# Moving two of three modulation sums from TensorE to VectorE in a hybrid decoder layer

## The chip, the cores and the metric

The kernel runs on one core of a Trainium2 chip. The core has five engines with queues of their own, each worked through in order: TensorE (PE, matrix products; its weight loads are shown as PEld), VectorE (DVE), ScalarE (ACT), GpSimd (POOL) and SyncE (SP), which here issues all transfers from the chip's memory. The metric is the device time of one execution in microseconds; lower is better.

## The reference, cut to what matters

One layer of a decoder: 256 tokens of width 2048. A conditioning vector c gives six modulations of 2048 numbers each, by one product of silu(c) with a matrix of 2048 x 12288:

```python
mod = (silu(c) @ w_mod + b_mod).reshape(B, 6, D)
sh1, sc1, g1, sh2, sc2, g2 = [mod[:, i, None, :] for i in range(6)]

h = rmsnorm(x, norm_mix) * (1.0 + sc1) + sh1
proj = h @ w_in                       # inputs of four mixers
y = concat([gla, gated_deltanet, pooling, forgetting_attention]) @ w_out
x = x + g1 * y

h = rmsnorm(x, norm_ffn) * (1.0 + sc2) + sh2
x = x + g2 * conv_ffn(h)              # gate, up: 2048 x 5632; down: 5632 x 2048
out = rmsnorm(x, norm_final)
```

Everything is float32. The first two modulations are needed at once. g1 is needed when the output projection is done, sc2 and sh2 at the second norm, g2 at the very end. This case is about when, and on which engine, the middle ones (g1, sc2, sh2) are summed.

## The kernel before, in words

Large products are made from split operands: each block of weights (128 x 1024 numbers, tile wr) is cut by ScalarE into a high part (wh) and by VectorE into the rest (wl), and three products of the parts stand for one product in float32. `load_split` (line 158) does one load and its split. The buffers allow five wr, three wh and three wl at a time.

The layer goes through these stages. First, the modulations sh1 and sc1 are summed in four groups while the input projection for DeltaNet follows group by group (tile acc). The projections for the other mixers, called `extras`, go by pairs of column blocks (tile ext); the last group of them, 25 steps, runs beside the mixers. The function `gated_deltanet` is traced first and so comes first where engines are contended; then, in the order "gpfd", the extra projections that a mixer needs and the mixer itself: GLA, pooling, attention (`fox`), and the finish of DeltaNet. Their products are in the tiles gdt (DeltaNet) and oxt (the others). Then comes the output projection, in five column chunks (`project`, three of 512 and two of 256 wide; 32 loads in all; sums in ext, oxt, wot, ext and oxt), then the second norm and the feed-forward part (tile fpt), which takes the second half of the time.

One half modulation is 1024 columns and is called by a letter and a number: s is sc2, h is sh2, g is g1; s0 is the first half of sc2. `gemv` (line 178) sums one, in eight steps of two loads of 512 KB each (tile wm, four buffers, shared by both ways). There are two ways:

- On TensorE: four matmuls per step with the conditioning number as weights of 32 columns, into the PSUM tile bgt, of which there is one. ScalarE copies the sums to a wr buffer and eight short products with `sel` finish them.
- On VectorE: two instructions `ga = wm * cond + ga` over 128 x 1024 per step (line 103, from line 174), into the SBUF tile ga, of which there is one. Then products with `ones` sum over the partitions: eight short ones for s and h, or four of 512 columns for g, which make a row.

Lists say which half goes which way, and rates how many steps of each are traced per step of the extra projections:

```python
ON_PE, PE_RATE = "s0 s1 h0", 0.38
ON_DVE, DVE_RATE = "h1 g0 g1", 0.69
```

`paced` gives out these steps. What is left of both lists is traced after the mixers, the TensorE list first (the flush). A g half has a condition before its row is formed: its mixer (GLA for g0, attention for g1, whose value tiles gv and fv the rows take over) must have been traced, and the TensorE list must be finished ("s" in `emitted`). Until then a step of it does nothing.

The order on every engine is fixed when the program is built. A planner goes through the instructions by priority, which is the order of tracing except where `high_priority` lifts the end of a modulation, and starts each on a simulated clock when its inputs and a buffer are there. So a step traced at one place fills gaps that lie near it. The transfers of the modulations are held behind an earlier one on SyncE's queue (`issue_after`), and are otherwise put into that queue in the planned order.

Of the kernel before, what the change touches and what calls it, by code (L numbers as in the profile page):

```python
# [49 lines left out]

ORDER = "gpfd"

ON_PE, PE_RATE = "s0 s1 h0", 0.38
ON_DVE, DVE_RATE = "h1 g0 g1", 0.69


def _consts():
# [16 lines left out]
def trunk_kernel(ctx: ExitStack, tc: tile.TileContext, x, c, w_mod, b_mod, norm_mix, norm_ffn, w_in,  # L74
# [36 lines left out]
    def act(o, a, f, **kw):  # L111
        S_.activation(o, a, f, **kw)
# [115 lines left out]
    with ExitStack() as ph:  # L228
# [59 lines left out]
        with ExitStack() as st:  # L288
# [184 lines left out]
                    yield from pair(p, done[p], g + 1)  # L473
                    done[p] = g + 1

            def jobs(seq, pst):
                col = pst or (ext)
                for job in seq.split():
                    kind, n = job[0], int(job[1])
                    k0, col0 = 8 * n, dict(s=4, h=3, g=2)[kind] * D + n * 1024  # L480
                    if kind == "s":
                        yield from gemv(col0, to_col(s2, 4, k0, nffn, col), pst)
                    elif kind == "h":
                        yield from gemv(col0, to_col(sh2, 3, k0, None, col), pst)
                    else:
                        yield from gemv(col0, g1_row(n, bgt), None,
                                        lambda: "gf"[n] in emitted and "s" in emitted, b_mod[:, col0:col0 + 1024])
# [3 lines left out]
            def marked(steps):  # L491
                yield from steps
                emitted.add("s")
# [10 lines left out]

            bgt = lambda: bgp.tile([P, 512], F32, name="bgt", tag="bgt")
            bg = [marked(jobs(ON_PE, bgt)), jobs(ON_DVE, None)]
            for _ in mods(0):
                pass
            hold = [last_wm[0]]
# [334 lines left out]
                finish(onl[t], t, nw_gla, 4, oxt().rearrange("p (h n) -> p h n", n=P))  # L844


        def fox(fp):
            ft_ = lambda shape, name, bufs=1: fp.tile(shape, F32, name=name, tag=name, bufs=bufs)
            fq, fk = pr[:, 16:20], pr[:, 20:24]
            for h in range(4):  # L850
                la = ft_([P, 3, P], "la", 2)
                for i, (m_, t) in enumerate(((K(K_LE), 0), (K(K_LE), 1), (ones, 0))):
                    act(la[:, i], m_, AF.Copy, scale=fl[:, t, h:h + 1])
                pT = oxt()
                ptv = pT[:, 0:3 * P].rearrange("p (a n) -> p a n", n=P)
                for t in range(NT):
                    n = (t + 1) * P
                    b = oxt()
                    mm(b[:, 0:n], fq[:, h, t * P:t * P + P], fk[:, h, 0:n], stop=False)
                    if t == 0:  # L860
                        mm(b[:, 0:n], la[:, 0], K(K_GT), start=False, stop=False)
                    else:
                        mm(b[:, 0:n], la[:, 1], K(K_ONE, 2 * P), start=False, stop=False)
                        mm(b[:, 0:P], la[:, 2], K(K_GT), start=False, stop=False)
                    mm(b[:, n - P:n], idr, ngr, start=False)
                    p = ft_([P, 2 * P], "p", 3)
                    s4 = ft_([P, 4], "s4", 3)
                    V.tensor_reduce(out=s4[:, 0:1], in_=b[:, 0:n], axis=AX.X, op=ALU.max, negate=True)
                    act(p[:, 0:n], b[:, 0:n], AF.Exp, bias=s4[:, 0:1], accum_out=s4[:, 1:2])
                    V.reciprocal(out=s4[:, 2:3], in_=s4[:, 1:2])  # L870
                    act(p[:, 0:n], p[:, 0:n], AF.Copy, scale=s4[:, 2:3])
                    for kk in range(t + 1):
                        PE.transpose(ptv[:, t + kk if kk == 0 else 2], p[:, kk * P:kk * P + P], ident)
                pt = ft_([P, 3, P], "pt", 2)
                S_.copy(pt, ptv)
                b = oxt()
                hs = slice(h * P, h * P + P)
                mm(b[:, 0:T], fv[:, 0, hs], flat(pt[:, 0:2]), stop=False)
                mm(b[:, P:T], fv[:, 1, hs], pt[:, 2], start=False)
                S_.copy(fq[:, h], b[:, 0:T])  # L880


        def pooling(pp):
            pw = pp.tile([P, 4, P], F32, name="pw")
            nc.sync.dma_start(pw, pool_w[0].rearrange("g c d -> c g d"))
            u = pr[:, 12:16]
            sa, sb = pp.tile([P, 4, T], F32, name="sa"), pp.tile([P, 4, T], F32, name="sb")
            cur, nxt = u, sa
            for li in range(4):
                sh = 1 << li  # L890
                S_.copy(nxt[:, li:, 0:sh], cur[:, li:, 0:sh])
                tt(nxt[:, li:, sh:], cur[:, li:, sh:], cur[:, li:, 0:T - sh], ALU.add)
                w = 2 * sh
                dl = pp.tile([P, T], F32, name="dl", tag="dl", bufs=2)
                hd = pp.tile([P, 16], F32, name="hd", tag="hd", bufs=2)
                stt(dl, nxt[:, li], 1.0 / w, u[:, li], ALU.mult, ALU.subtract)
                tt(hd, nxt[:, li, 0:16], K(K_INV + 16 * li, 16), ALU.mult)
                tt(dl[:, 0:16], hd, u[:, li, 0:16], ALU.subtract)
                b = oxt()
                mm(b[:, 0:T], pw[:, li], dl)  # L900
                act(u[:, li], b[:, 0:T], AF.Copy, scale=pscale[:, li:li + 1])
                cur, nxt = nxt, (sb if nxt is sa else sa)
# [44 lines left out]
        chunks = ((0, 512), (512, 512), (1024, 512), (1536, 256), (1792, 256))  # L947
        Y2 = bigA()

        def project(n, a):  # L950
            c0, w = chunks[n]
            nk = 1024 // w
            for j in range(KT // nk):
                ks = order[nk * j:nk * j + nk]
                if n == 0:
                    for k in ks:
                        split(Y2[:, k, 0:T], Y2[:, k, T:], pr[:, k + 4])
                wh, wl = load_split(wo_v, ks[0], nk, c0, w)
                steps = [(kk, k, t) for kk, k in enumerate(ks) for t in range(NT)]
                if n == len(chunks) - 1 and ks[-1] == order[-1]:  # L960

                    steps.sort(key=lambda s: s[2])
                for kk, k, t in steps:
                    st, sp_ = j + kk == 0, nk * j + kk == KT - 1
                    xh, xl = Y2[:, k, t * P:t * P + P], Y2[:, k, T + t * P:T + t * P + P]
                    mm(a[t], xh, wh[:, kk], start=st, stop=False)
                    mm(a[t], xh, wl[:, kk], start=False, stop=False)
                    mm(a[t], xl, wh[:, kk], start=False, stop=sp_)
# [12 lines left out]
        with tc.tile_pool(name="op", bufs=2, reuse_waits="tile") as op:  # L981
            for n, (c0, w) in enumerate(chunks):
# [6 lines left out]
                for t in range(NT):  # L989
                    m_ = op.tile([P, 512], F32, name="m_", tag="m_")[:, 0:w]  # L990
                    tt(m_, a[t], g1t[c0 // 1024][:, gs], ALU.mult)
                    tt(x1[:, t, ns], x1[:, t, ns], m_, ALU.add)
                    act(m_, x1[:, t, ns], AF.Square, accum_out=x1s[:, t, n:n + 1])


    with ExitStack() as ph:
# [150 lines left out]
```

## Time and profile before

| | |
|---|---|
| median of 3 runs | 1301.3 us (1297.34 to 1302.14) |
| the profiled execution | 1299.62 us |
| its span, first to last instruction | 1297.8 us |
| mean granted TensorE clock | 0.985 |
| TensorE busy | 1243.1 us (96%) |
| TensorE weight loads busy | 1075.8 us (83%) |
| VectorE busy | 889.1 us (69%) |
| ScalarE busy | 636.2 us (49%) |
| moved by DMA | 311.91 MB, mean 240 GB/s |

The profile is one execution. Busy times of an engine are sums over its instructions. A row of a group gives line, engine, operation, output tile and input tiles, shapes and count, then busy time in us and the mean of one in ns, then the idle time just before them and what ended it. "A <- B" in the view of waits means that A waited for B, with total us, times and the longest. The chain of work that ended last is followed back from the last instruction, at each step to what released it.

### The profile page before, as it was taken

Reading aid. Unit: us, or ns where it says so; the run is one execution under the profiler, and the core shown is the slowest. Engines: PE = TensorE matmul, PEld = TensorE weight load, DVE = VectorE, ACT = ScalarE, POOL = GpSimd, SP = SyncE. Lnnn points to the kernel's source line nnn. Section 1 sums busy time; section 2 is a strip of 40 time slices with the busy share of each in tenths; the row PEclk is TensorE's granted clock in tenths of the full one; section 3 lists DMA queues with packets and bytes.
Section 4 is the critical chain, followed back from the end, with each engine's and each line's share of the span. In section 5 each row is a group of like instructions: output and inputs, shape, how many; then the busy total and the mean of one; then the engine's idle time right before and its main releaser. Section 6 shows DMA issues by size and latency. Waiting matters only on the chain.

```text
span 1297.8 us, 19845 instructions
## 1 busy us (share of the span) xinstructions
PE 1243.1 (96%) x7663; PEld 1075.8 (83%) x7663; DVE 889.1 (69%) x1201; ACT 636.2 (49%) x1000; POOL 23.1 (2%) x31
## 2 busy tenths in 40 slices
PE   2799999999999999999999999999999999999995
PEld 1799999898876688888888888888888888888884
DVE  7679797989763397676657666665666587964543
ACT  3455344774354454564545545554545444443432
POOL 0200000010000100000000000000000000000000
PEclk9799999999999999999999999999999999999998
DMA  9899999796567898556576666657665699875552
GB/s 326 274 367 377 333 333 302 255 334 227 163 231 248 306 330 279 155 165 192 163 212 193 179 196 194 182 172 209 186 191 165 212 364 379 307 259 184 193 194 81
DMA packets 168597, 311.91 MB, mean 240 GB/s; under 512 B 16172, under 2 KB 54067, under 8 KB 167863
## 3 DMA queue, kind: packets, MB, share of 16 engines
q1 hardware_dynamic: 168503, 310.65, 73.0%
q8 instruction: 60, 0.98, 0.3%
q14 instruction: 34, 0.28, 0.1%
HBM read 308.51 MB, written 2.10 MB: 239 GB/s over the span
## 4 chain that ended last, share of the span: by engine, by line
PE 91%; DMA 4%; SPq 1%; DVE 1%; ACT 1%; issue 1%; POOLq 0%; ACTq 0%; DVEq 0%
PE fpt L97 57%; PE ext L97 16%; PE oxt L97 5%; PE acc L97 4%; PE gdt L97 4%; DMA wm<-in_w_mod_dram 3%; PE bgt L97 3%; PE wot L97 2%; DMA wr<-in_w_in_dram 1%; DVE ga L103 1%; ACT xT L1015 0%; SPq L155 0%; SPq L399 0%; DVE m L100 0%; DVE wl L100 0%
## 5 line engine op out<-in xcount | busy, mean ns | idle before, releaser
L100 DVE TENSOR_TENSOR wl<-wr,wh 128x1024 fp32r<-128x1024 f32 x384 | 469.4, 1223 | 293.7 <-ACT wh L115 292.9
L115 ACT CAST wh<-wr 128x1024 fp32r<-128x1024 f32 x384 | 403.6, 1051 | 489.5 <-PE fpt L97 316.5
L97 PE MATMUL fpt<-bigA,wh 128*128 128x512 f32 x1408 | 399.6, 396 | 2.1 <-DVE bigA L103 2.1
L97 PEld LDWEIGHTS fpt<-bigA,wh 128*128 128x128 f32 x1408 | 239.2, 189 | 32.9 <-issue 2.2
L97 PEld LDWEIGHTS fpt<-bigA,wl 128*128 128x128 f32 x1408 | 222.6, 188 | 34.2 <-DVE wl L100 3.7
L97 PE MATMUL fpt<-bigA,wl 128*128 128x256 f32 x1408 | 240.5, 279 | 0.0
L103 DVE SCALAR_TENSOR_TENSOR ga<-wm,cond,ga 128x1024 f32<-128x1024 f32 x139 | 178.1, 1281 | 11.5 <-DMA wm<-in_w_mod_dram 10.6
L97 PE MATMUL fpt<-wl,AH 128*128 128x512 f32 x352 | 137.5, 391 | 0.0
L97 PE MATMUL ext<-bigA,wh 128*128 128x256 f32 x768 | 137.3, 281 | 0.0
L97 PE MATMUL fpt<-wh,AL 128*128 128x512 f32 x352 | 137.0, 389 | 0.0
L97 PE MATMUL fpt<-wh,AH 128*128 128x512 f32 x352 | 123.5, 390 | 0.0
L97 PEld LDWEIGHTS ext<-bigA,wh 128*128 128x128 f32 x768 | 117.5, 189 | 3.0 <-DVE dS L100 0.8
L97 PE MATMUL ext<-bigA,wl 128*128 128x256 f32 x384 | 107.4, 280 | 1.7 <-DVE wl L100 1.7
L97 PE MATMUL ext<-wh,bigA 128*128 128x256 f32 (+1 forms) x384 | 79.3, 300 | 0.0
L97 PEld LDWEIGHTS fpt<-wh,AH 128*128 128x128 f32 x352 | 66.1, 188 | 14.1 <-ACT wh L115 0.2
L97 PEld LDWEIGHTS fpt<-wl,AH 128*128 128x128 f32 x352 | 66.1, 188 | 13.9 <-DVE m L100 0.2
L97 PEld LDWEIGHTS fpt<-wh,AL 128*128 128x128 f32 x352 | 66.1, 188 | 13.8 <-issue 0.2
L97 PE MATMUL acc<-bigA,wh 128*128 128x256 f32 x384 | 70.1, 289 | 4.6 <-ACT bigA L115 2.7
L97 PEld LDWEIGHTS ext<-bigA,wl 128*128 128x128 f32 x384 | 72.1, 188 | 2.8 <-DVE wl L100 1.9
L97 PEld LDWEIGHTS ext<-wh,bigA 128*128 128x128 f32 x384 | 61.6, 188 | 5.5 <-ACT wh L115 1.7
L97 PEld LDWEIGHTS acc<-bigA,wh 128*128 128x128 f32 x384 | 60.7, 199 | 5.0 <-ACT bigA L115 2.8
L97 PE MATMUL ext<-wl,bigA 128*128 128x256 f32 (+1 forms) x192 | 58.3, 304 | 1.6 <-DVE wl L100 1.6
(344 smaller groups left out, 1172.1 us busy)
## 6 DMA issues: line engine op xcount, KB each, us to landing
wm<-in_w_mod_dram SPq DMA_DIRECT2D x192, 512.0 KB, 5.7
wr<-in_w_in_dram SPq DMA_DIRECT2D x88, 512.0 KB, 9.1
wr<-in_ffn_w_gate_dram SPq DMA_DIRECT2D x88, 512.0 KB, 3.9
wr<-in_ffn_w_up_dram SPq DMA_DIRECT2D x88, 512.0 KB, 4.4
wr<-in_ffn_w_down_dram SPq DMA_DIRECT2D x88, 512.0 KB, 4.4
wr<-in_w_out_dram SPq DMA_DIRECT2D x32, 512.0 KB, 4.8
xt<-in_x_dram SPq DMA_DIRECT2D x2, 1024.0 KB, 7.1
bigC<-in_x_dram SPq DMA_DIRECT2D x2, 1024.0 KB, 12.2
```

Of the source, the lines that this page charges most:

```text
L97: PE.matmul(o, lhsT=l, rhs=r, start=start, stop=stop, skip_group_check=True)
L100: V.tensor_tensor(out=o, in0=a, in1=b, op=op)
L103: V.scalar_tensor_tensor(out=o, in0=a, scalar=s, in1=b, op0=op0, op1=op1)
L115: S_.copy(hi, src)
```

## The change: what it does

The list of TensorE keeps s0, at a rate of 0.25 steps per step of the extra projections in place of 0.38. The half s1 joins VectorE's list behind h1; the rate of that list stays. New places give out steps of that list: two before each of the four attention heads, one before each of the four steps of pooling. The half h0 is summed on VectorE during the output projection: from the second column chunk on, one of its eight steps is traced at every third load of output weights; its column sums go through the tile bgt. Nothing else of the computation is changed.

```diff
-ON_PE, PE_RATE = "s0 s1 h0", 0.38
-ON_DVE, DVE_RATE = "h1 g0 g1", 0.69
+ON_PE, PE_RATE = "s0", 0.25
+ON_DVE, DVE_RATE = "h1 s1 g0 g1", 0.69
+LATE, LATE_LOADS = "h0", 3
...
-            def jobs(seq, pst):
-                col = pst or (ext)
+            def jobs(seq, pst, col=None):
+                col = col or pst or ext
...
             bg = [marked(jobs(ON_PE, bgt)), jobs(ON_DVE, None)]
+            late = jobs(LATE, None, bgt)
...
+        def beside(n):
+            with tc.issue_after(hold[0].ins):
+                for _ in range(n):
+                    next(bg[1], None)
+
         def fox(fp):
...
             for h in range(4):
+                beside(2)
...
         def pooling(pp):
...
             for li in range(4):
+                beside(1)
...
+        wo_loads = [0]
+
         def project(n, a):
...
                 wh, wl = load_split(wo_v, ks[0], nk, c0, w)
+                wo_loads[0] += 1
+                if n > 0 and wo_loads[0] % LATE_LOADS == 0:
+                    next(late, None)
...
+        for _ in late:
+            pass
```

## The prediction

> **What bounds the kernel now.** I read the engine totals first, then the chain of work that ended last, then the busy time stage by stage, and last who issues and who waits in the stages that the change touches.
>
> ```profile
> span 1297.8 us, 19845 instructions
> PE 1243.1 (96%) x7663; PEld 1075.8 (83%) x7663; DVE 889.1 (69%) x1201; ACT 636.2 (49%) x1000; POOL 23.1 (2%) x31
> PE 91%; DMA 4%; SPq 1%; DVE 1%; ACT 1%; issue 1%; POOLq 0%; ACTq 0%; DVEq 0%
> PE fpt L97 57%; PE ext L97 16%; PE oxt L97 5%; PE acc L97 4%; PE gdt L97 4%; DMA wm<-in_w_mod_dram 3%; PE bgt L97 3%; PE wot L97 2%; DMA wr<-in_w_in_dram 1%; DVE ga L103 1%; ACT xT L1015 0%; SPq L155 0%; SPq L399 0%; DVE m L100 0%; DVE wl L100 0%
> ```
>
> TensorE sets the end: 91% of the chain is its work. Its modulations (tile bgt) hold 3% of that chain, about 40 us. Nothing else that the change touches has as much to give. The next question is whether TensorE is full where bgt stands. The columns are busy time and count by engine, granted clock, share of the DMA engines, rate.
>
> ```profile
> core 0: us, PE busy (x) PEld busy (x) DVE busy (x) ACT busy (x) POOL busy (x), PEclk, DMA share, GB/s
> 245.00:381.00 136.00, 135.39 (x1105) 118.75 (x1108) 112.77 (x175) 70.82 (x141) 6.74 (x4) 1.00 0.72 242
> 381.00:445.00 64.00, 63.53 (x427) 40.07 (x416) 24.15 (x70) 29.39 (x84) 1.01 (x1) 1.00 0.78 261
> 445.00:462.00 17.00, 17.00 (x84) 13.32 (x82) 10.00 (x17) 12.80 (x32) 2.75 (x2) 1.00 0.98 372
> 462.00:505.00 43.00, 43.00 (x190) 35.32 (x189) 42.43 (x42) 19.50 (x26) 0.00 (x0) 1.00 0.92 334
> 505.00:541.00 36.00, 36.00 (x249) 32.92 (x249) 19.98 (x22) 15.82 (x22) 0.96 (x1) 1.00 0.63 189
> by line: PE bgt L97 40.1%; PE gdt L97 31.7%; PE oxt L97 15.4%; DMA wm<-in_w_mod_dram 6.1%; PE oxt L873 2.8%; PE gdt L672 1.7%; PE gdt L661 1.4%; PE gdt L656 1.3%; PE gdt L735 0.4%; issue 0.1%
> ```
>
> Stage 1 (245 to 381) has the last extra input projections, GLA and the first half of DeltaNet. Stage 2 (381 to 445) has the rest of DeltaNet, pooling and most of the attention, and no projection matmuls at all. Stage 3 (445 to 541) is the output projection. TensorE is full in all three. The last line is the chain from 381 to 448: bgt is its largest single part, 40.1%. VectorE is busy for 24.15 of 64 us there, so there is room for the moved work just where TensorE has none.
>
> **The change, part by part.** *What leaves TensorE.*
>
> ```profile
> L97 PE MATMUL bgt<-wm,cond 128*32 128x512 f32 x192 | 38.0, 603 | 1.1 <-DMA wm<-in_w_mod_dram 1.1
> L97 PE MATMUL bgt<-wm,cond 128*32 128x512 f32 x120 | 24.5, 603 | 0.5 <-DMA wm<-in_w_mod_dram 0.5
> L97 PE MATMUL bgt<-sel,wr 128*128 128x1 f32 x32 | 3.9, 252 | 0.0
> ```
>
> The first row is all three jobs; the other two are of stage 2 alone. A job has 8 steps of two loads, so 192 records are 24 steps of 8. Stage 2 holds 120 of them, 15 steps at 24.5/15 = 1.63 us; stage 1 the other 9 steps at (38.0 - 24.5)/9 = 1.50 us. That agrees with the pace in the code: 25 steps of extra projections (counted from the loop) times 0.38 is 9.5, so 9 steps are paced and 15 are left for the flush. With one job at 0.25, 6 steps are paced and 2 flushed. So stage 1 loses 3 steps, 4.5 us, and stage 2 loses 13, 21.2 us: **25.7 us** of TensorE in all (two thirds of 38.0 gives 25.3). The short column sums (bgt<-sel, 3.9/2 us a job) stay: s1 and h0 need the same eight products from ga and ones. The two copies of bgt to wr vanish on ScalarE, which is not full.
>
> *What VectorE gets.* Two jobs of 16 accumulations each.
>
> ```profile
> core 0: us, PE busy (x) PEld busy (x) DVE busy (x) POOL busy (x), PEclk, DMA share, GB/s
> 245.00:381.00 136.00, 1.95 (x16) 1.86 (x16) 33.32 (x26) 0.96 (x1) 1.00 0.72 242
> 381.00:445.00 64.00, 0.00 (x0) 0.00 (x0) 0.00 (x0) 0.00 (x0) 1.00 0.78 261
> 445.00:541.00 96.00, 4.09 (x8) 1.49 (x8) 20.49 (x16) 1.90 (x2) 1.00 0.82 286
> L103 DVE SCALAR_TENSOR_TENSOR ga<-wm,cond,ga x16: 1277/1280/1285, 462.6 to 503.6; 128x1024 f32<-128x1024 f32 x16
> L97 PE MATMUL bgt<-ga,ones x8: 591/592/594, 445.7 to 515.1; 128*128 128x512 f32 x8
> POOL ga L179 <- PE bgt L97: 61.3, 1, 61.3
> ```
>
> These are the windows of the tile ga alone. One accumulation takes 1.28 us, so the two jobs add 32 x 1.28 = 41 us to VectorE. Now h1 and g0 run in stage 1 and g1 runs from 462.6 to 503.6. In between there is nothing for 61.3 us: the one ga buffer holds g0 until its row is formed, and that waits for the flush of TensorE's three jobs (the code marks "s" only then). With 2 steps to flush instead of 15, g0's row can be formed soon after 381, and g1 can move into stage 2.
>
> The order is then: 17 paced steps and 4 in pooling (h1, s1, part of g0), then the first steps before the attention heads finish g0 (of the 8 offered there, some find g0 already waiting), then g1 in the flush. In stage 1 the paced amount is the same 17 steps, and 136 - 112.77 = 23 us are free, enough for four more steps (10 us). Stage 2 gets about 8 accumulations of g0 and 16 of g1, 31 us on top of 24.15: 55 us.
>
> *The late job, h0.* Its 8 steps stand at every third of the 24 loads behind the first column chunk, so it adds 16 x 1.28 = 20.5 us to stage 3, which is what g1 (20.49 us) leaves if it moves forward.
>
> ```profile
> 472.70:494.70 22.00, 22.00 (x98) 18.07 (x97) 21.46 (x21) 9.79 (x12) 0.00 (x0) 1.00 1.01 375
> ```
>
> This window is the second chunk, 8 loads of weights. VectorE is 97.5% busy with about one accumulation per load, DMA moves 375 GB/s, and TensorE misses nothing. The late job asks for two accumulations per three loads, less than that. I cost it at 0. If g1 stayed where it is, h0 could not begin before the last row product has read ga, at 515.1; then 20.5 us come onto the 19.98 in 505 to 541, 40.5 in 36, and the second norm starts 4.5 us late. So the bounds are 0 and +4.5, and I take 0 because the row that runs denser costs nothing. The additions to the projection's SyncE queue are 16 loads of wm among 24 of wr; the row above has the same mixture.
>
> *What stage 2 really gives back.* If TensorE alone set it, 64 us would shrink by 21.2 to 42.8. Two things can hold it longer. The first is the loads.
>
> ```profile
> 381.50 56.94 SPq L185 DMA_DIRECT2D wm<-in_w_mod_dram  x30
> 438.49 5.01 SPq L155 DMA_DIRECT2D wr<-in_w_out_dram  x5
> wm<-in_w_mod_dram SPq DMA_DIRECT2D x192, 512.0 KB, 5.7
> DMA to landing us min/median/max: 3.6/4.8/8.1
> ```
>
> SyncE issues 30 wm loads there and only then the first load of the output weights. After the change: 4 loads for TensorE, about 8 for g0, 16 for g1 and 8 of output weights for the first chunk, 36 x 0.524 MB = 18.9 MB. At the 375 GB/s of the row above that is 50 us, so stage 2 can shrink by 14 at most before the loads bind, unless g1 spills into stage 3, where there is room. The second is the two chains, DeltaNet's and the attention's, each of which passes TensorE, then VectorE or ScalarE, and TensorE again; without filler TensorE waits in them. There is new filler: half of the first chunk (GLA's and pooling's heads, 4 of 8 loads, half of 22 us = 11 us) needs neither chain, and with the 26 wm loads gone from ahead of it, its weights can come early. The bounds of stage 2's gain are 0 (only chains) and 21.2 (only TensorE); I take **14**, the loads' bound, which also leaves TensorE 7 us of waits.
>
> The trace shows what empty stretches can do to the clock:
>
> ```profile
> 545.00:549.00 4.00, 1.81 (x10) 1.51 (x11) 2.70 (x7) 3.06 (x8) 0.00 (x0) 1.00 0.34 117
> 549.00:553.00 4.00, 4.00 (x17) 3.40 (x16) 2.26 (x5) 2.12 (x5) 0.00 (x0) 0.57 0.00 0
> ```
>
> After four microseconds at 1.81 busy, the granted clock was 0.57 in the next four. Stage 2 would have 7 idle us spread over some 40 hops, far from 1.81 of 4, so I add nothing; one such dip costs about 4 x 0.43 = 1.7 us. [...]
>
> *Sum.* Stage 1: -4.5, of which VectorE at 112.77 of 136 may keep 1.5, so -3. Stage 2: -14. Stage 3: 0. Together **-17 us**. The profiled execution took 1299.62 us, of which 1297.8 span; less 17 it is 1282.6. The median of the runs is 1.7 above it, so **1284 us** is the forecast.
>
> **The rivals.** *Full gain.* TensorE sets everything, as its 63.53 of 64 us suggest: the whole 25.7 comes back, 1301.3 - 25.7 = 1276. The filler of 11 us speaks for it, the loads against. Chance 0.12.
>
> *The chains set stage 2.* The bgt pieces only fill what DeltaNet and the attention leave open; taken away, TensorE idles there. For it: weight loads are busy for 40.07 of 64 us in stage 2 against 118.75 of 136 in stage 1. Against it stands the chain itself, in order of time (start, length):
>
> ```profile
> 424.67 0.99 PE bgt L97 x8
> 425.66 1.02 PE gdt L97 x8
> 426.68 0.98 PE bgt L97 x4
> ...
> 429.07 1.08 PE gdt L97 x8
> 430.16 0.99 PE bgt L97 x8
> 431.15 0.58 PE gdt L97 x4
> 431.73 0.98 PE bgt L97 x4
> ```
>
> DeltaNet's pieces (gdt) each have a bgt piece of about 1 us ahead of them or behind, so the chains may well wait for bgt. In this case only stage 1's 3 to 4.5 us are left, 1297. [...] Chance 0.17.
>
> *VectorE stands in the chains' way: slower.* VectorE's queue is in order. An accumulation whose wm is late holds DeltaNet's and the attention's operations queued behind it, and TensorE behind those.
>
> ```profile
> DVE ga L103 <- DMA wm<-in_w_mod_dram: 2.9, 4, 1.6
> ```
>
> Before, such waits are 2.9 us in stages 1 to 3. The 30 loads of stage 2 came every 56.94/30 = 1.9 us, with four buffers and 4.8 us to land; at this pace a step of two takes 3.8 us, of which VectorE works 2.56 and could wait 1.24. Over the 14 steps of wm in stage 2 that is 17 us put onto chains which, in this case, no longer gain from bgt's absence. Less stage 1's 4.5 that is +12.5: 1314. It decides once these waits pass 4.5 us, and it shows from 11. Chance 0.10.
>
> **How the numbers follow.** The forecast's own case (gain 10 to 23, 1278 to 1291) gets 0.61. What a measurement of this kernel tells from no change is about 0.5%, 6.5 us. Forecast and full gain are faster by more: 0.73; of the chains' case (gain 0 to 9) 0.05 is faster, 0.11 within, 0.01 slower; of the slower case 0.01 is within and 0.09 slower. So faster 0.78, same 0.12, slower 0.10. The range goes from 1274, just under the full gain, to 1299, which takes in the chains' case and leaves out the slower one.
>
> **What would show it.** Right: the group bgt<-wm,cond has 64 records and some 12 to 13 us; ga runs at 381 to 445 where its window was empty, and its last 16 accumulations, of h0, lie among the output projection; the first output weights are issued well before 438, and projection matmuls (ext<-wh,bigA) stand between DeltaNet's; TensorE stays at 95% or more from the end of the extra projections to the second norm. Wrong: if TensorE falls to 70% in that stretch with releasers DVE or ACT, the chains set it; if VectorE's waits for wm pass 10 us, the slower case; if g1 still ends near 500 after the shift, h0 crowds the end of stage 3 and the second norm starts late.

## The result and the profile after

| | before | after |
|---|---|---|
| median of 15 runs each | 1301.15 us (1297.34 to 1303.63) | 1313.82 us (1300.73 to 1317.44) |
| ratio, 95% interval | 1 | 1.0082 [1.0065, 1.0099] |
| TensorE busy, profiled execution | 1243.1 us | 1224.1 us |
| VectorE busy, profiled execution | 889.1 us | 923.9 us |
| span and clock of the profiled execution | 1297.8 us, 0.985 | 1299.0 us, 0.980 |

The kernel became 0.8% slower, where 1.3% faster was forecast; the time lies outside the range. One thing has to be known for reading the profile: the profiled execution of the changed kernel is the quickest of its 15, 13 us under their median. It shows what became of the work; what the other executions lost is seen only beside a second profile of the same kernel (the first experiment). Medians and intervals in this document leave out four executions whose whole program ran far slower (one of f1's ten, 2069.78 us at a clock of 0.556, one of f2's nine, 1566.75 us at 0.742, and two of the kernel before beside e1 to e4).

The totals of the changed kernel's page, and the shares of its chain of waits by engine:

```profile
span 1299.0 us, 19653 instructions
PE 1224.1 (94%) x7535; PEld 1073.5 (83%) x7535; DVE 923.9 (71%) x1233; ACT 636.2 (49%) x998; POOL 22.7 (2%) x31
PE 76%; DMA 9%; DVE 8%; ACT 3%; issue 2%; SPq 1%; POOL 0%; ACTq 0%; POOLq 0%; DVEq 0%
```

TensorE does 19 us less and the span is no shorter: its share of the chain fell from 91% to 76%, and DMA and VectorE now hold 17%. The same five stretches as in the prediction (busy time and count by engine, granted clock, DMA share, rate):

```profile
245.00:381.00 136.00, 129.51 (x1065) 118.99 (x1065) 120.65 (x185) 71.86 (x141) 6.84 (x4) 0.97 0.76 243
381.00:445.00 64.00, 56.55 (x353) 44.65 (x352) 52.89 (x93) 32.03 (x77) 0.98 (x2) 0.97 0.85 289
445.00:462.00 17.00, 11.29 (x61) 8.04 (x56) 9.94 (x23) 10.29 (x35) 2.03 (x2) 1.00 0.78 295
462.00:505.00 43.00, 41.54 (x177) 33.08 (x178) 39.81 (x39) 19.05 (x26) 0.00 (x0) 1.00 0.82 293
505.00:541.00 36.00, 36.00 (x267) 33.84 (x267) 19.91 (x25) 15.30 (x21) 0.95 (x1) 1.00 0.63 190
```

TensorE was full in all of them before. Now it stands empty for 6.5 us in stage 1, 7.5 in stage 2, 5.7 in the next 17 us and 1.5 in the 43 behind: 21 us, where 27.6 us of bgt left it. The accumulations on VectorE (tile ga alone, without ScalarE's column) moved the way that the prediction gave:

```profile
core 0: us, PE busy (x) PEld busy (x) DVE busy (x) POOL busy (x), PEclk, DMA share, GB/s
245.00:381.00 136.00, 3.69 (x32) 3.73 (x32) 44.09 (x35) 0.95 (x1) 0.97 0.76 243
381.00:445.00 64.00, 2.15 (x4) 0.60 (x4) 23.03 (x18) 0.95 (x1) 0.97 0.85 289
445.00:541.00 96.00, 4.09 (x20) 2.53 (x20) 23.78 (x19) 0.95 (x1) 1.00 0.74 255
```

Stage 2, which held none, holds 18 (about 24 were given). The group of TensorE's modulations, the output weights' issues on SyncE's queue, and the waits of VectorE's accumulations for their loads (245 to 541) follow, each from its own view:

```profile
L99 PE MATMUL bgt<-wm,cond 128*32 128x512 f32 x64 | 10.4, 603 | 3.7 <-DMA wm<-in_w_mod_dram 3.7
```

```profile
401.70 1.41 SPq L157 DMA_DIRECT2D wr<-in_w_out_dram  x3
```

```profile
DVE ga L105 <- DMA wm<-in_w_mod_dram: 6.3, 5, 2.7
```

64 records are left, the output weights start 37 us sooner (401.70 against 438.49), and VectorE waits 6.3 us for loads against 2.9. In this execution the second norm's first instruction stood at 545.3 us, against 545.8 before. Everything was moved as described, and nothing was gained.

### The profile page after: what moved, and what is told of

It reads as the page before. It is cut to its first block, busy times and chain, and to the rows that moved or that the text cites. A ratio compares the mean times of both kernels' runs of the same rounds, so it can differ in the third digit from the quotient of the medians.

```text
span 1299.0 us, 19653 instructions
## 1 busy us (share of the span) xinstructions
PE 1224.1 (94%) x7535; PEld 1073.5 (83%) x7535; DVE 923.9 (71%) x1233; ACT 636.2 (49%) x998; POOL 22.7 (2%) x31
## 4 chain that ended last, share of the span: by engine, by line
PE 76%; DMA 9%; DVE 8%; ACT 3%; issue 2%; SPq 1%; POOL 0%; ACTq 0%; POOLq 0%; DVEq 0%
PE fpt L99 57%; PE ext L99 10%; DMA wm<-in_w_mod_dram 4%; DMA wr<-in_w_in_dram 4%; PE oxt L99 3%; DVE ga L105 3%; PE acc L99 2%; DVE wl L102 2%; PE gdt L99 2%; PE wot L99 2%; DMA wr<-in_w_out_dram 1%; ACT wh L117 1%; DVE xt L105 1%; PE bgt L99 1%; DMA wsm<-in_w_in_dram 0%
## 5 line engine op out<-in xcount | busy, mean ns | idle before, releaser
L105 DVE SCALAR_TENSOR_TENSOR ga<-wm,cond,ga 128x1024 f32<-128x1024 f32 x169 | 216.1, 1279 | 15.3 <-DMA wm<-in_w_mod_dram 13.0
```

The source lines that it names most:

```text
L105: V.scalar_tensor_tensor(out=o, in0=a, scalar=s, in1=b, op0=op0, op1=op1)
```

## The experiments

Ratios are against the kernel before, on the same chip. The clock and the span are medians over the runs of each kernel; the last column is worked out (see "One kernel, twice").

| run | what differs | us | ratio [95%] | clock | span | span at 0.985 |
|---|---|---|---|---|---|---|
| before | | 1301.15 | | 0.985 | 1299.3 | 1299 |
| after | | 1313.82 | 1.0082 [1.0065, 1.0099] | 0.969 | 1312.0 | 1296 |
| e1 | the changed kernel again | 1311.79 | 1.0085 [1.0058, 1.0111] | 0.968 | 1310.0 | 1293 |
| e2 | s1's part alone | 1326.28 | 1.0188 [1.0153, 1.0223] | 0.967 | 1324.5 | 1307 |
| e3 | h0's part alone | 1300.48 | 0.9993 [0.9974, 1.0011] | 0.9815 | 1298.7 | 1295 |
| e4 | s1 and h0 left out | 1299.75 | 0.999 [0.9972, 1.0008] | 0.980 | 1297.9 | 1293 |
| e5 | after, with empty TensorE steps | 1331.53 | 1.0215 [1.0193, 1.0238] | 0.972 | 1329.8 | 1317 |
| e6 | short accumulations of s1 and h0 | 1301.05 | 0.9989 [0.9974, 1.0004] | 0.9795 | 1299.3 | 1294 |
| e7 | TensorE's rate back at 0.38 | 1301.25 | 0.999 [0.9977, 1.0003] | 0.976 | 1299.5 | 1291 |
| e8 | e4, with empty TensorE steps | 1306.88 | 1.0038 [1.0019, 1.0057] | 0.982 | 1305.1 | 1302 |
| e9 | s0 and s1 on TensorE, rate 0.64 | 1308.69 | 1.0049 [1.0026, 1.0072] | 0.981 | 1306.9 | 1303 |
| e10 | before, with 21 forced gaps | 1468.09 | 1.1288 [1.1258, 1.1318] | 0.940 | | |
| e11 | rates 0.38 and 0.48 | 1302.53 | 1.0011 [0.9998, 1.0024] | 0.977 | 1300.75 | 1293 |
| e12 | before, TensorE's rate 0.25 | 1308.37 | 1.0067 [1.0043, 1.009] | 0.984 | 1306.6 | 1306 |
| f1 | rates 0.25 and 0.48 | 1306.94 | 1.0047 [1.0028, 1.0065] | 0.974 | 1305.2 | 1294 |
| f2 | no steps between attention and pooling | 1306.78 | 1.0043 [1.0029, 1.0057] | 0.974 | 1305.0 | 1294 |
| f3 | rates 0.38 and 0.58 | 1303.57 | 1.0018 [1.0003, 1.0033] | 0.977 | 1301.8 | 1294 |
| f4 | rates 0.50 and 0.58 | 1304.24 | 1.002 [1.0006, 1.0034] | 0.9775 | 1302.4 | 1295 |

**One kernel, twice.** e1 is the changed kernel with no edit.

> The changed kernel once more, to see a profile of an ordinary execution: its own profile took 1300.7 us, while its runs had a median of 1313.8 and their granted clock fell with their time (0.980 at a span of 1299.0, 0.964 to 0.972 at 1308 to 1316). Theory A, the clock: TensorE's waits in the stages of the mixers let the granted clock dip; an execution near 1313 shows more or longer stretches below 1.00 between 245 and 560 us, the same busy times of the other engines, and a time that is longer by about its loss of mean clock times the span. Theory B, VectorE's queue alone: the time differs between executions because VectorE's waits for loads differ; an execution near 1313 shows some 13 us more of DVE waits for wm, and the clock is a by-product.

The loss repeats, and the clock goes with it. Over the 21 executions of the changed kernel in both sets of runs, spans run from 1299.0 us at a clock of 0.980 to 1315.7 at 0.966, on a straight line of -984 us per 1.0 of clock (correlation -0.94). The last column of the table is the median span moved to 0.985 with this slope; it is an extrapolation, no measurement. It is good to some 3 us at best: the same kernel comes out at 1296 in one set and at 1293 in the other, and the slopes within other kernels differ (-933 in e4, -539 in e6, -765 in e7). e1's profiled execution had a span of 1315.3 us. Around the place where it parts from the other one, first in the profile of the first run, then in e1's (same columns as above):

```profile
320.00:324.00 4.00, 3.90 (x37) 3.64 (x36) 4.00 (x8) 1.70 (x4) 0.00 (x0) 1.00 0.84 253
324.00:328.00 4.00, 1.46 (x13) 1.49 (x14) 4.00 (x7) 0.95 (x3) 0.00 (x0) 1.00 0.31 74
328.00:332.00 4.00, 3.19 (x30) 2.81 (x28) 4.00 (x7) 2.81 (x6) 0.00 (x0) 1.00 0.40 115
...
340.00:344.00 4.00, 4.00 (x28) 3.75 (x29) 2.74 (x7) 0.42 (x1) 0.95 (x1) 0.73 0.40 129
```

```profile
324.00:328.00 4.00, 1.91 (x20) 1.65 (x18) 4.00 (x6) 1.30 (x4) 0.00 (x0) 0.88 0.43 144
328.00:332.00 4.00, 3.47 (x16) 3.49 (x16) 3.94 (x7) 0.59 (x1) 0.00 (x0) 0.50 0.43 135
332.00:336.00 4.00, 4.00 (x22) 3.67 (x21) 1.78 (x3) 1.89 (x5) 0.00 (x0) 0.50 0.42 131
336.00:340.00 4.00, 4.00 (x23) 3.66 (x21) 3.22 (x8) 0.62 (x2) 0.00 (x0) 0.50 0.42 131
340.00:344.00 4.00, 4.00 (x18) 3.77 (x19) 3.43 (x5) 1.60 (x4) 0.00 (x0) 0.50 0.71 186
344.00:348.00 4.00, 4.00 (x38) 3.93 (x37) 2.99 (x6) 1.39 (x3) 0.00 (x0) 0.93 0.64 207
348.00:352.00 4.00, 4.00 (x20) 3.78 (x20) 0.85 (x4) 0.00 (x0) 0.95 (x1) 0.50 0.00 1
352.00:356.00 4.00, 4.00 (x23) 3.88 (x23) 2.90 (x3) 0.59 (x1) 0.00 (x0) 0.50 0.14 22
356.00:360.00 4.00, 4.00 (x19) 3.66 (x18) 1.73 (x2) 1.69 (x3) 0.00 (x0) 0.50 0.71 245
360.00:364.00 4.00, 4.00 (x31) 3.82 (x30) 1.99 (x3) 1.05 (x1) 0.00 (x0) 0.86 0.40 133
364.00:368.00 4.00, 4.00 (x32) 3.59 (x30) 3.87 (x7) 1.63 (x5) 0.00 (x0) 1.00 0.43 131
```

Both lose TensorE for over 2 us at 324 to 328, and VectorE is busy throughout. TensorE's longest wait on VectorE at 320 to 332 is the same, for the tile W of DeltaNet (total, times, longest; again the first run's profile, then e1's):

```profile
PE gdt L99 <- DVE W L639: 2.6, 1, 2.6
```

```profile
PE gdt L99 <- DVE W L639: 3.4, 2, 2.6
```

In the first the clock stays at 1.00 behind it and is 0.73 and 0.84 in two later windows (340 to 348). In e1 it is 0.50 in seven of the nine windows from 328 to 364, though TensorE is busy for 4.00 of 4 from 332 on: x16 to x23 instructions in such a window, against x32 at 364, at 1.00. Taking each window's length times what its clock lacks to 1.00, 324 to 364 lost 15.3 us of clock in e1 and 1.7 us in the first, and the last matmul of the extra projections starts at 399.6 against 387.0, 12.6 us later. Over 184 to 620 the lost clock is 28.9 against 8.5 us, a difference of 20.4; the spans differ by 16.3. Before, the same sum was 1.7 us. VectorE's waits for wm are 5.4 us in e1 and 6.3 in the first, so late loads are not what sets the two apart. The difference between two executions of this kernel is clock. What sets it off is not shown: the fall in e1 begins at a gap, but the quicker execution has the longer idle time at the same place (2.54 against 2.09 of 4 us) and kept 1.00, and f1 below shows a fall without any gap.

Summed over windows of 4 us, the falls lose close to whole multiples of 1.7 us of clock: 1.72, 1.72, 1.68 and, at 544 to 556, 3.40 in the first profile; 15.32 at 324 to 364 and else 1.68, 1.72, 1.68, 3.40 and 3.40 up to 548 in e1's; 5.12 at 308 to 324 in f1's and 6.84 at 324 to 344 in e7's. What sets this length is not shown.

**The two parts apart, and no work at all.** e2 leaves h0 on TensorE and sums only s1 on VectorE, with the steps between; e3 does only h0 beside the output projection.

```diff
 e2
-ON_PE, PE_RATE = "s0", 0.25
+ON_PE, PE_RATE = "s0 h0", 0.25
-LATE, LATE_LOADS = "h0", 3
+LATE, LATE_LOADS = "", 3
 e3
-ON_PE, PE_RATE = "s0", 0.25
-ON_DVE, DVE_RATE = "h1 s1 g0 g1", 0.69
+ON_PE, PE_RATE = "s0 s1", 0.38
+ON_DVE, DVE_RATE = "h1 g0 g1", 0.69
-                beside(2)
-                beside(1)
 e4
-ON_DVE, DVE_RATE = "h1 s1 g0 g1", 0.69
-LATE, LATE_LOADS = "h0", 3
+ON_DVE, DVE_RATE = "h1 g0 g1", 0.69
+LATE, LATE_LOADS = "", 3
-                beside(2)
-                beside(1)
+            tt(s2[:, 8:16], bm(4, 8, 8), nffn[:, 8:16], ALU.mult)
+            V.tensor_copy(sh2[:, 0:8], bm(3, 0, 8))
```

> s1 goes to VectorE with the steps between attention and pooling; h0 stays in TensorE's list (rate 0.25), nothing is late. Theory A: TensorE keeps 8 steps of filler, some 12 us, so it waits less and the clock dips less; time 1300 to 1306. Theory B: VectorE is overloaded from 300 to 400 us by the added steps of s1, so this part carries the loss: 1308 or more. My forecast's mechanism, were it right, gives 1301 less about 8, 1293.

> h0 goes to VectorE beside the output projection; s0 and s1 stay on TensorE at the old rate (0.38), and no steps stand in attention and pooling. Theory B: VectorE's load ahead of 445 us is that of before, so the 12 us of TensorE come back: 1290 to 1294. Theory A: as VectorE does not hold TensorE up in the mixers, little is lost there; 1290 to 1300, with a clock near that of before. The rival that DeltaNet's and the attention's chains set the stage gives 1298 to 1303, with TensorE idle where h0 was.

> Removal alone: s1 and h0 are not summed at all (the second half of sc2 and the first half of sh2 are made from their biases alone), so 64 accumulations, matmul steps and 32 loads are missing and nothing replaces them. If only TensorE's work set the mixers' stages: 1301 - 26 = 1275. If the chains set them: about 1297, TensorE idle for some 20 us between 380 and 445. Theory A adds to that the clock: with TensorE idle for 15 us or more there the granted clock falls below that of before and the time comes out above 1290 although 2 x 8 steps are gone.

e3 costs nothing and gains nothing, although TensorE has eight steps less to do. e2 is slower by 1.9%, more than both parts together; the theory of VectorE's queue gave 1308 or more, the clock theory 1300 to 1306, and neither gave this size. About 18 of its 25 us go with its clock of 0.967; the other 8 stand beside e12's 7 (the kernel before at the same rate of 0.25), but why the clock falls further than with both parts is not settled.

e4 says most. It takes the whole 25.7 us off TensorE and leaves VectorE's total as before (888.6 us against 889.1), and the time is the same. Its page's totals, two stretches, and the waits of TensorE in 381 to 505 (total, times, longest):

```profile
PE 1225.7 (94%) x7503; PEld 1070.9 (82%) x7503; DVE 888.6 (68%) x1200; ACT 636.1 (49%) x998; POOL 22.4 (2%) x31
```

```profile
381.00:445.00 64.00, 52.50 (x314) 41.78 (x313) 48.35 (x90) 29.34 (x88) 2.87 (x4) 0.95 0.49 153
445.00:505.00 60.00, 52.65 (x214) 41.66 (x215) 26.82 (x40) 27.45 (x52) 1.35 (x2) 0.89 0.39 135
```

```profile
PE oxt L884 <- ACT p L114: 5.9, 3, 3.3
PE ext L99 <- ACT bigA L117: 3.6, 4, 1.4
PE gdt L99 <- DVE bigC L102: 2.0, 1, 2.0
PE gdt L666 <- DVE bigC L102: 2.0, 1, 2.0
```

TensorE is empty for 18.9 of 124 us there, VectorE is busy for 75 of 124 and the DMA share is under a half. These waits and the shorter ones, 18.7 us together, are all for results of ScalarE and VectorE in the chains of attention (p, the splits into bigA) and DeltaNet (bigC), at a clock of 0.95 and 0.89. The extra projections' last matmul starts 20 us earlier than before (360.2 against 380.2), the attention's last instruction on p 9 us later (462.1 against 452.7). So this stretch is not set by the sum of TensorE's work, and the removed steps were filler between dependent operations.

Two more things differ in e4. TensorE's rate is 0.25, which by itself costs the kernel before 7.2 us (e12, where the last p starts at 463.3). And g0 and g1 move forward, so VectorE is busy for 48.35 of 64 us in stage 2 against 24.15 before. The removal at the old rate was not run; e3 is at the old rate, has half of the removal, and gains nothing either.

**VectorE's load.** e6 keeps every load, wait and step of s1 and h0 but sums 128 of 1024 columns; the other columns of their rows repeat those.

```diff
-                    accumulate(acc, wm, k + kk, bias is None)
+                    if part:
+                        accumulate(acc[:, 0:P], wm[:, 0:P], k + kk, bias is None)
+                    else:
+                        accumulate(acc, wm, k + kk, bias is None)
...
```

> The changed kernel, but the accumulations of s1 and h0 take 128 of their 1024 columns (the other columns of sc2 and sh2 repeat them); every load stays, VectorE loses some 32 x 1.1 = 35 us. Theory B: VectorE's added time was the cause, so the time falls to that of the kernel in which s1 and h0 are not summed at all, 1300. Theory A: TensorE still idles in the mixers, as it did with nothing summed; the time is about 1300 too, with the clock near 0.975, and it is this 0.975 and not VectorE that keeps it from 1290. If the loads were the cause: 1310 or more.

1301.05 us: without VectorE's time the loss is gone, as in e4, and again there is no gain. At equal clock e6 is 2 us below the changed kernel and e4 is 3 us below, but so is e1, the changed kernel itself. What the accumulations cost at equal clock is therefore not resolved; the loss goes with the clock.

**Rates and places.** e7 gives the last job on TensorE its old rate; f1 lowers VectorE's rate; e11, f3 and f4 do both; f2 takes the steps between out of attention and pooling; e9 keeps s1 on TensorE at a rate that paces both jobs; e12 only lowers the rate in the kernel before.

```diff
 e7, on the changed kernel
-ON_PE, PE_RATE = "s0", 0.25
+ON_PE, PE_RATE = "s0", 0.38
 f1, on the changed kernel (e11, f3, f4: 0.38/0.48, 0.38/0.58, 0.50/0.58)
-ON_DVE, DVE_RATE = "h1 s1 g0 g1", 0.69
+ON_DVE, DVE_RATE = "h1 s1 g0 g1", 0.48
 f2, on the changed kernel
-                beside(2)
-                beside(1)
 e9, on the changed kernel, the steps between removed as in f2
-ON_PE, PE_RATE = "s0", 0.25
-ON_DVE, DVE_RATE = "h1 s1 g0 g1", 0.69
+ON_PE, PE_RATE = "s0 s1", 0.64
+ON_DVE, DVE_RATE = "h1 g0 g1", 0.69
 e12, on the kernel before
-ON_PE, PE_RATE = "s0 s1 h0", 0.38
+ON_PE, PE_RATE = "s0 s1 h0", 0.25
```

> The changed kernel with one number put back: the rate of TensorE's list 0.38 in place of 0.25, so that s0 is finished among the extra projections instead of in the flush. Theory A: TensorE has more to do ahead of 381 us, dips there (268 to 276, 324 to 364 us in the two profiles) become fewer: 1303 to 1309. Theory B: no change, 1311 to 1316.

> Only h0 goes to VectorE, beside the output projection; s0 and s1 stay on TensorE at a rate of 0.64, so that all their 16 steps are paced among the extra projections and none is left for the flush (with 0.38 and 7 steps in the flush this kernel took 1300.5). Theory A, the clock: TensorE stays full ahead of 381 us and what it does there is paid in full; g0's row and g1 come earlier, and the stage from 381 to 445 has no filler, so the clock dips there: 1297 to 1303. If only the waiting for g0's row held g1 and h0 up: 1290 to 1295.

> The change with TensorE's rate at 0.38 and VectorE's rate lowered from 0.69 to 0.48, so VectorE gets 12 paced steps in place of 17 and is less full from 300 to 345 us. Theory A with VectorE's load as the cause of the gaps: fewer dips from 324 to 344 us than in the kernel with 0.38 and 0.69 (1301.3, clock 0.976), 1294 to 1299. If the later end of g1 then pushes h0 against the second norm: 1302 to 1310.

> The kernel before with one number changed: TensorE's rate 0.25 in place of 0.38; the three jobs stay on TensorE, 18 of 24 steps come in the flush. Theory A in its simplest form (a lower rate starves TensorE ahead of 381 us and the clock dips): 1308 to 1315 with a clock of 0.970 to 0.978. If the rate matters only together with the added load of VectorE: 1299 to 1304 with the clock of before.

> The change with one number different: VectorE's rate 0.48 in place of 0.69 (12 paced steps in place of 17), TensorE's rate still 0.25. In both profiles of the change VectorE is 30.00 of 30 us busy from 300 to 330 and TensorE idles 3.4 to 3.6 us there; in one of them the granted clock then stays near 0.5 until 364. If VectorE's fullness from 300 to 330 opens that gap and the gap costs the clock: no dip between 320 and 364, clock 0.975 to 0.978, time 1300 to 1304. If the lower rate of TensorE does it by itself: 1308 to 1315 as with 0.69.

> The change without the steps between attention and pooling (what they would have given out is left to the flush); all else as changed. If these steps stand in the chains' way (the slower case of my prediction): faster than the change by some 5 to 10 us, 1303 to 1308, with less VectorE work from 345 to 400. If the loss arises ahead of them, from 300 to 330: the same as the change, 1311 to 1316.

> The change with rates 0.38 and 0.58. With 0.38 and 0.69 the time was 1301.3 with a dip from 324 to 344 (6.8 us of clock) and none at 440 to 468; with 0.38 and 0.48 it was 1302.5 with no dip from 324 to 344 but one from 444 to 468. If a rate between avoids both: 1291 to 1296, faster than the kernel before. If one of the two dips stays: 1299 to 1303.

> The change with rates 0.50 and 0.58: s0 is through some four steps of the extra projections earlier, so TensorE has more to do ahead of 330 us and nothing of s0 is left beside GLA's end. If a full TensorE at 300 to 330 is what keeps the clock: no dip there, 1292 to 1299. If only the gaps after 381 count: 1300 to 1304.

e7 undoes the whole loss: 12.6 us, of which the clock (0.976 against 0.969) is 7 by the slope; the rest goes with the order of the steps or lies in the error of the slope. Its stretches:

```profile
300.00:330.00 30.00, 27.02 (x216) 23.02 (x215) 27.15 (x38) 13.26 (x18) 0.00 (x0) 0.96 0.67 218
381.00:445.00 64.00, 58.06 (x375) 51.22 (x371) 58.64 (x98) 36.94 (x79) 0.95 (x1) 0.95 0.85 296
445.00:505.00 60.00, 55.97 (x271) 44.70 (x270) 49.31 (x66) 29.06 (x67) 2.01 (x2) 0.97 0.79 281
```

VectorE is no longer full in 300 to 330 (27.15 of 30), and TensorE still is empty in every stretch, for 3 us in this one. f1 (-6.9) and f2 (-7.0), at the rate of 0.25, take off about half of the loss by moving VectorE's work to later places. e11, f3 and f4 have e7's rate or a higher one, and at 1302.5 to 1304.2 VectorE's lower rates add nothing to what e7 gains. None goes below the kernel before.

f1's profile speaks against a simple story of gaps. TensorE has no wait from 276 to 328, VectorE is busy for 26.57 of 30 us in 300 to 330, and the clock falls all the same:

```profile
308.00:312.00 4.00, 4.00 (x34) 3.76 (x34) 3.17 (x9) 2.55 (x7) 0.00 (x0) 0.99 0.63 231
312.00:316.00 4.00, 4.00 (x23) 3.78 (x23) 3.08 (x5) 0.00 (x0) 0.00 (x0) 0.50 0.48 142
316.00:320.00 4.00, 4.00 (x20) 3.88 (x20) 4.00 (x7) 0.72 (x2) 0.00 (x0) 0.50 0.72 226
```

What stands just ahead are the sixteen one-column products that end a sum on VectorE (ext<-ones,ga, 310.0 to 311.8). They also stand just ahead of the falls at 340 in the changed kernel's first profile, at 348 in e1's, at 356 in f2 and at 302 in f3. But at 292.7 before, the same products were followed by 1.00, so they are a suspect and no shown cause.

e12 shows that the rate has a price of its own without a drop of clock (0.984): more of the steps are left for the flush, and the kernel before loses 7.2 us. e9 at a clock of 0.981 loses 7.5, so pacing everything early is no remedy either.

Several of these times were not expected. e7 is better than both of its cases, e9 worse than both, and f1 lies between its two. f3 and f4 come out just above the ends (1303 and 1304) of the cases in which a fall of the clock stays. e12 has the time of one case and the clock of the other. f2's 1306.78 is what was expected if the steps between stand in the chains' way.

**Filler put back.** e5 adds to the changed kernel 16 empty steps on TensorE (4 in the paced part, 12 in the flush); e8 adds them to e4. Both have the rate of 0.38, e4 that of 0.25.

```diff
-ON_PE, PE_RATE = "s0", 0.25
+ON_PE, PE_RATE = "s0", 0.38
+FILL = 12
...
+            def filler():
+                for _ in range(FILL):
+                    b = bgt()
+                    for c in range(4):
+                        mm(b[32 * c:32 * c + 32], cond[:, c:c + 1].to_broadcast([P, 32]),
+                           ct[:, c % 2 * 448:c % 2 * 448 + 512])
+                    yield
...
-            for b_ in bg:
+            for b_ in (bg[0], filler(), bg[1]):
```

> The changed kernel with TensorE's load given back as empty work: 16 steps of four matmuls of the same shape, without loads and without a use (4 with zero weights between the steps of s0, paced as before at 0.38, and 12 offered with the flush). VectorE's work and all loads are those of the change. Theory A, the clock: the gaps in TensorE are filled, the granted clock comes back to about 0.98, and adding 25 us of useless work makes the kernel faster than the change: 1298 to 1305. Theory B, VectorE: it changes nothing in what TensorE waits for, 1311 to 1317. If TensorE's own work set the end, 1313 + 25.

> s1 and h0 not summed at all, with the same empty work of 16 steps on TensorE. Theory A: the clock returns to about 0.985; as the mixers' chains take the same time with or without filler, the time is 1295 to 1300, not above that without filler (1299.8). If TensorE's work counted in full: 1299.8 + 25. If it comes out far below 1295, the loads of wm (32 of them, absent here) were what the kernel before paid for.

The clock theory's expectation failed here: e5 is 17.7 us slower than the changed kernel, not quicker, and 30.3 us slower than e7, which has e5's rate of 0.38 and no empty steps. e8 is 7.1 us slower than e4. By its time e5 comes nearest to the case in which TensorE's own work is paid for in full (1338). A likely reading is the place: filler that stands in one piece ahead of the flush holds back what follows. In e5 the last accumulation on VectorE begins 63 us later than in e7 (567.3 against 504.5):

```profile
L106 DVE SCALAR_TENSOR_TENSOR ga<-wm,cond,ga x72: 1267/1278/1287, 255.1 to 567.3; 128x1024 f32<-128x1024 f32 x72
```

No run has the empty steps in another place, so this reading is not shown. The clock in e5 is below e7's (0.972 against 0.976), in e8 a little above e4's (0.982 against 0.980). So these two runs don't show that filler as such pays.

**What a gap costs.** e10 ties the first split of each chunk of gate and up weights to the last chunk's product in the kernel before, which makes 21 gaps on a TensorE that is full there.

```diff
+                if g == 0 and prev[0] is not None:
+                    wr = load(view, 0, 2, c0, 512)
...
+                    with tc.high_priority():
+                        stt(wr[:, 0, 0:1], prev[0], 0.0, wr[:, 0, 0:1], ALU.mult, ALU.add)
+                        split(wh[:, 0:2], wl[:, 0:2], wr[:, 0:2])
+                else:
+                    wh, wl = load_split(view, 2 * g, 2, c0, 512)
...
+            prev[0] = a[3][:, T:T + 1]
```

> The kernel before with 21 controlled gaps on TensorE in the feed-forward stage and nothing else: the first block of weights of each gate or up chunk but the first is split only when the chunk ahead is through (a 1-column instruction that adds zero ties it), so TensorE waits some 2 to 4 us there. Theory A: each gap is followed by a stretch at about 0.5 of the clock, and the kernel loses more than the idle time: for 21 gaps of 3 us, 63 us idle and some 20 to 60 us more, with the mean granted clock down from 0.985 to 0.94 to 0.97. If gaps of this length do not move the clock: the loss equals TensorE's idle time and the clock stays at 0.98.

One gap by windows of 4 us, and the group whose last column holds the waits for the tied splits (wh):

```profile
600.00:604.00 4.00, 2.30 (x14) 1.84 (x13) 1.60 (x5) 1.72 (x6) 0.00 (x0) 1.00 0.00 0
604.00:608.00 4.00, 0.00 (x0) 0.00 (x0) 3.55 (x10) 2.33 (x6) 0.00 (x0) 0.76 0.00 0
608.00:612.00 4.00, 2.43 (x7) 2.05 (x8) 3.46 (x7) 3.41 (x5) 0.00 (x0) 0.50 0.06 6
612.00:616.00 4.00, 4.00 (x22) 3.50 (x21) 2.24 (x2) 1.05 (x1) 0.00 (x0) 0.88 0.91 296
616.00:620.00 4.00, 4.00 (x25) 3.49 (x24) 1.26 (x2) 1.76 (x2) 0.00 (x0) 1.00 0.70 225
```

```profile
L97 PE MATMUL fpt<-bigA,wh 128*128 128x512 f32 x1408 | 419.0, 423 | 123.4 <-ACT wh L115 121.3
```

The 21 gaps hold 121.3 us, 5.8 each; 2 to 4 were expected. The kernel takes 167 us more than before, so 45 us, 2.2 for each gap, come on top of the waits, with the clock at 0.50 behind the gap shown: over a third of its length again. (The lost clock is more, about 3 us a gap in 550 to 950, where the clock is 0.90 on the mean and 13 gaps lie, but part of it falls into the gap, where nothing runs.) These gaps are over twice as long as the wait of 2.6 us at 324 in the changed kernel, so they show nothing about gaps of that length.

## Why the prediction was wrong

**What held.** 64 records and 10.4 us of bgt (12 to 13 were given), 19 us less on TensorE in the profiled execution (25.7 were given), accumulations in the empty stretch, the output weights at 401.70, h0's last accumulation at 501.5. The zero for h0 held in sum: e3, which moves h0 alone, is 0.9993 [0.9974, 1.0011]. None of the three signs of being wrong came as it was put: TensorE is busy for 88% of stage 2, neither 95 nor 70; VectorE's waits for wm are 6.3 us, above the 4.5 from which the slower case was to decide and under the 10 that were to show it; and g1's row is formed at 464, not near 500.

**"Stage 1 loses 3 steps", -3.** The term fell, and in this profile the bound had moved. In 300 to 330, the window and the chain by line, before and after:

```profile
300.00:330.00 30.00, 30.00 (x247) 26.37 (x246) 27.87 (x39) 14.23 (x20) 0.00 (x0) 1.00 0.70 231
by line: PE ext L97 50.0%; PE gdt L97 19.6%; PE oxt L97 18.2%; PE bgt L97 9.9%; PE gdt L626 2.9%
```

```profile
300.00:330.00 30.00, 26.40 (x229) 24.27 (x228) 30.00 (x43) 16.09 (x25) 0.00 (x0) 1.00 0.73 243
by line: issue 19.1%; DMA wr<-in_w_in_dram 15.8%; DVE ga L105 14.5%; DVE wl L102 13.7%; DVE dd L102 8.2%; DVE at L790 7.9%; DVE pr L102 4.7%; DVE E L102 4.4%; DVE qE L102 3.4%; DVE W L639 2.5%; DVE X L630 2.4%; DVE Y L631 2.1%; DVE at L102 
```

Before, the chain ran through TensorE alone, with VectorE at 27.87 of 30. After, VectorE is 30.00 of 30 and the chain passes its accumulations (ga), weight splits (wl) and DeltaNet's W. "23 us are free" was read over 136 us; here 2 were. The accumulations in this window are 7 against 8 before, so there aren't more of them; that the extra projections, and with them their splits, follow each other more closely when TensorE has less between them is a reading. A full VectorE alone doesn't open the gap: in e12 it is 30.00 of 30 in this window too, and TensorE keeps 30.00.

**"I take 14", stage 2.** This is the step that failed: no gain came. Of its two bounds, 0 for the chains and 21.2 for TensorE, the runs lie at the lower: e4 at 0.999 with none of the two halves' work anywhere, e3 at 0.9993 at the old rate. The mistake was to read TensorE's 63.53 of 64, and bgt's 40.1% of the chain, as proof that it set the stage, when they showed only that it was never empty. With the steps gone it stands empty for 18.9 us in waits for ScalarE and VectorE (e4). The sign that it might not was weighed and given too little: weight loads were 40.07 of 64 there. The new filler from the first chunk did come early, and TensorE still was 56.55 of 64, not the 95% named.

**"So I add nothing", the clock.** The largest error, 16 us: the median clock went from 0.985 to 0.969, and 0.016 x 984 is 15.7. The waits were taken as spread over some 40 hops of stage 2; the stretch from 324 to 364, in a stage where no loss was expected, alone lost 13.6 us more of clock in e1 than in the quicker execution. The dip that was costed there, 1.7 us from one row at 0.57, was the right kind of thing, but the forecast added none: e1 has seven falls from 188 to 620, and one of them lasts 36 us.

**The sum as measured.** In spans: 1299.3 before. Removal alone is -6 at equal clock (e4, 1293.0), the VectorE work in its place 0 to +3 (1293.3 to 1296.3, from the two sets of runs of the changed kernel), the clock +16 to +17: 1310.0 to 1312.0. The forecast had -17, 0 and 0. The first two are brought to one clock by the slope, so they are worked out and not shown directly; that e4, e6 and e7 each take the loss away is shown.

**The rivals.** The case of the chains (chance 0.17, 1297) names the term that failed; it lacked the clock. The slower case (0.10, 1314) has the number by luck. Its mechanism, 17 us of late loads, is not there: the waits for wm are 6.3 us, and 5.4 in e1's profile, which is 16 us longer. f2 speaks for it in part, as half of the loss goes with the steps between; but 5 of these 7 us go with the clock by the slope. What the runs show in its place is that the loss needs both VectorE's time for the two halves (it is gone in e6) and TensorE's rate of 0.25 (it is gone in e7), and that it comes with a lower clock. Full gain is out by e4.

**Open.** What lowers the clock: gaps stand ahead of most falls, but not of all, and not every gap is followed by one. What removal alone would give at the rate of 0.38. Why e5 pays for its empty steps, and why e2 is the slowest way to divide the halves. How the gain of e7 is split between order and clock other than by the slope.

## What to carry to other kernels

Work that an engine does between other chains' steps may be filler: before you pay for its removal, remove it for nothing (as in e4, but with every rate left as it was), since a TensorE that was 99% busy here (63.53 of 64 us) did not yet set the end. An engine's room has to be read in short windows too: VectorE had 23 us free in 136, and 2 in the 30 from 300 on. And where a change opens gaps on TensorE, compare the granted clock over many executions, as one profile can be the one that escaped (0.980 here, against a median of 0.969).

## What was not expected of the hardware

- Beside a wait of 2.6 us the clock fell to 0.50 in one execution and was there for most of some 36 us (one window at 0.93), with TensorE busy 4.00 of 4 from 332 on; with the same wait it kept 1.00 in another.
- In f1 the clock fell to 0.50 with TensorE busy 4.00 of 4 in every window from 276 to 328.
- The spread between executions of one kernel on one core grew from 6 us (1297.34 to 1303.63) to 17 us (1300.73 to 1317.44) in the first set of runs, on a line of -984 us per 1.0 of clock; in later sets the kernel before spread by up to 10.6 us (1296.65 to 1307.29).
- Forced gaps of 5.8 us each cost another 2.2 us each; behind the one of 7.3 us at 602 to 610 the clock was 0.50.
